# A one-tile lag behind the norm's mean, a low half moved behind four sums, and the last stores on two queues

## The chip, the cores and the metric

The kernel runs on one core of one Trainium2 chip. The metric is device time in microseconds (us) of one execution. A profile is one execution taken by the hardware profiler; it has times of its own. Engines: PE is TensorE (matmuls), DVE is VectorE, ACT is ScalarE, POOL is GpSimd, SP is SyncE. A name with a q (SPq, ACTq) is the engine's queue of transfers that it issues.

## The reference, cut to what matters

The model is one layer of a bidirectional encoder block, 1024 tokens by 1024 features, float32. Its first part (gated linear attention, a pooling branch and the gates that merge them) stands ahead of the change. The change lies in the rest:

```python
merged = jax.nn.sigmoid(g_a) * y_a + jax.nn.sigmoid(g_b) * y_b
x = x + merged @ w_out[l]                       # output projection
h2 = rmsnorm(x, norm_ffn[l])
gate, up = jnp.split(h2 @ w_ffn_in[l], 2, axis=-1)
x = x + (jax.nn.silu(gate) * up) @ w_ffn_out[l]  # gated sums
return rmsnorm(x, norm_final)
```

`rmsnorm` divides each token's row by the root of its mean square (plus 1e-6) and multiplies by a gain per feature.

## The kernel before, in words

**Products.** Every large product is split two ways. Each float32 operand is a high part, which ACT casts, and a low part, the difference, which DVE or POOL subtracts (`split_to`, L197 to 199). One step is then three matmuls of 128x128 by 128x512: high with high, high with low, low with high (`products`, L291). Above that, each product of 2 by 2 blocks is done in seven block products instead of eight (Strassen's scheme in Winograd's form); they are numbered 1 to 7 and their sums are collected block by block.

**Order.** The program is one list of instructions per engine, written out by hand; each engine works through its own in order. Small work is woven between the matmuls by `pump`, which counts matmul time and runs side generators and steps put off by `soon`.

**Output projection** (`project`, with `collect_out`, L1569). The block products run in the order 1, 4, 6, 7, 5, 2, 3. Each has two pieces c = 0, 1 of the contraction, and in each piece four groups of 128 tokens, m = 0 to 3, each with a PSUM bank of its own. Products 5, 2 and 3 start new sums (the argument `first`); three of their four banks are the same three buffers, so the first matmul of group m in one product waits until DVE has collected group m of the product before. After the last piece of group m, `collect_out` adds the bank to the residual row tile x2[t] (DVE, L1572). Rows 0 to 3 are finished in product 5, rows 4 to 7 in product 3. For a finished row tile ACT takes two sums of squares (`squares`, L1548), the tile joins the list `unnormed`, and `normed(1)` (L1562) is called, which handles all but the newest. For each tile it handles, it issues the mean's sum on DVE (L1554), the power of -0.5 on POOL (L1555), the scaling of the row tile by it on DVE (`scale_by`, L327), then the store of the tile before on SP's queue (`flush`, L500), and it lists the tile itself for the next store (`later`). Ahead of product 2 and at the end, `normed()` empties the list.

**Features.** `features(0)` starts in product 2 and `features(1)` after product 3: PE transposes the scaled tiles xn (L1503), four to a bank, ACT evicts them (L1506), ACT casts and POOL or DVE subtracts their low parts (L1484, L1488). The first of these transposes in a half reads all four tiles of that half.

**Gated sums.** The second FFN product also has seven block products in the order 1, 2, 6, 5, 3, 7, 4, each of six pieces along the contraction (`pieces`, 42 in all; the sixth is half as long). `load_piece` issues two loads, a weight w and the gated values g. `split_piece` (L1710) makes both parts of both, ACT casting, DVE taking the low part of w and POOL that of g. Splits run three pieces ahead: within each piece one is issued after the group m = 1, and two further ones behind m = 3 close to the end. Products 1, 6, 7 and 4 share the same four banks. With the last piece of product 7 (n = 35) `collect` adds each group to x2 (DVE, L1816), ACT squares that half, POOL multiplies it by the final gain (`second_half`, L1794). Product 4 closes: its first three pieces in the usual order, then for each m the last three, the sum, and `first_half` (L1801): squares, mean, power, the left half scaled on DVE (L1805), the right half on ACT (L1808), and two stores on SP's queue (L1810).

Of the kernel before, what the change touches and what calls it, by code (L numbers as in the profile page):

```python
# [17 lines left out]
P = 128  # L18
# [34 lines left out]
def kernel(  # L53
# [20 lines left out]
    nc = tc.nc  # L74
    x, out = x[0], out[0]
# [20 lines left out]
    def slot(dtype=F32, shape=(2, HALF), s="slot"):  # L96
        return slots.tile([P, *shape], dtype, tag="slot", name=name(s))
# [7 lines left out]
    def vec(width, s="v"):  # L105
        return small.tile([P, width], F32, tag="vec", name=name(s), bufs=12)

    def bank(pool, s="ps"):
        return pool.tile([P, HALF], F32, tag=pool.name, name=name(s))

    def as_f32(ap):
        return ap.bitcast(F32)
# [8 lines left out]
        out=keepf[:, :P], in_=keepf[:, :P], compare_op=ALU.is_ge, fill=0.0,  # L121
        base=0, pattern=[[1, P]], channel_multiplier=-1,
    )
    keep = const.tile([P, 4, P], U8, tag="keep", name="keep")
# [30 lines left out]
    def settle():  # L155
        while put_off:
            put_off.pop(0)[1]()
# [39 lines left out]
    def split_to(hi, lo, src, eng=nc.vector):  # L197
        nc.scalar.copy(hi, src)  # L198
        eng.tensor_tensor(lo, src, as_f32(hi), op=ALU.subtract)  # L199
# [93 lines left out]
    def mm3(ps, a, b, first, last, onto=False):  # L293
        products(ps, a, b, first, last, onto)
        pump(ps.shape[-1] / HALF)
# [30 lines left out]
    def scale_by(dst, src, rs):  # L326
        nc.vector.tensor_scalar(dst[:, :], src, rs[:, :], None, op0=ALU.mult)  # L327
# [35 lines left out]
    xn = [slot(shape=(D,), s="xn") for _ in range(4)]  # L363
# [131 lines left out]
    def later(dst, src):  # L495
        deferred.append((dst, src))

    def flush(eng=nc.sync):
        while deferred:
            eng.dma_start(*deferred.pop(0))  # L500
# [13 lines left out]
    sub = partial(nc.vector.tensor_tensor, op=ALU.subtract)  # L514
# [917 lines left out]
    x2 = [None] * NT  # L1432
# [12 lines left out]
    xn = [None] * NT  # L1445
# [99 lines left out]
    COLS = slice(0, HALF), slice(HALF, D)  # L1545

    def squares(t, ms, res, j):
        nc.scalar.activation(  # L1548
            res[:, COLS[j]], x2[t][:, COLS[j]], AF.Square, scale=1.0 / 32.0, accum_out=ms[:, j : j + 1]
        )  # L1550

    def two_scale(ms):
        rs = vec(1, "n3rs")
        nc.vector.tensor_scalar(rs[:, :], ms[:, 0:1], ms[:, 1:2], EPS, op0=ALU.add, op1=ALU.add)  # L1554
        nc.gpsimd.tensor_tensor(rs[:, :], rs[:, :], half_neg[:, :1], op=ALU.pow)  # L1555
        return rs

    mss = {}

    unnormed = []  # L1560

    def normed(keep=0):  # L1562
        while len(unnormed) > keep:
            t = unnormed.pop(0)
            scale_by(xn[t], x2[t][:, :], two_scale(mss[t]))
            flush()
            later(x2_out[t], x2[t][:, :])

# [15 lines left out]
    def before_out(p):  # L1584
        if p == 2:
            normed()
            begin(features(0), 11.5)
        elif p == 5:
            for _ in range(2):
                units[2].load()  # L1590
        elif p == 3:
            for _ in range(2):
                units_ahead.step()
# [102 lines left out]
    def load_piece():  # L1696
        if len(loaded_pieces) == len(pieces):
            return
        p, q, c = pieces[len(loaded_pieces)]
        g, w = slot(s="gor"), slot(s="wor")  # L1700
        if p in RAW_B:
            i, j = RAW_B[p]
            src = w_ffn_out[(i * PAIRS + q) * P : (i * PAIRS + q + c) * P, j * HALF : (j + 1) * HALF]
            nc.sync.dma_start(w[:, :c, :], src.rearrange("(q p) c -> p q c", p=P))
        else:
            nc.sync.dma_start(w[:, :c, :], t_out[p][:, q : q + c, :])
        nc.sync.dma_start(g[:, :c, :], g_out[p][:, q : q + c, :])
        loaded_pieces.append((w, g))

    def split_piece():  # L1710
        n = len(ready_pieces)
        if n == len(pieces):
            return
        while len(loaded_pieces) <= n:
            load_piece()
        c = pieces[n][2]
        both = []
        for src, eng in zip(loaded_pieces[n], (nc.vector, nc.gpsimd)):
            hi, lo = slot(F32R, s="oh"), slot(F32R, s="ol")
            split_to(hi[:, :c, :], lo[:, :c, :], src[:, :c, :], eng)  # L1720
            both.append((hi, lo))
        ready_pieces.append(both)

# [6 lines left out]
    for n, run in enumerate(unit_runs, 1):  # L1730
# [7 lines left out]
        for at, (of, p) in enumerate(run):  # L1738
            while n == 1 and p > 2 and p not in split_done:
                next(side[0][0])  # L1740
            units_ahead.step()
            zs[of].run(p)
            if (of, p) in ((0, 3), (1, 3)):
                units[3].load()
            elif 2 < n < FT - 1 and at in (1, 2):
                units[n + 1].load()
            if n > 1 and 0 < at + (n == 2) < 6:
                next(summing, None)
            if n == FT - 1:
                for what in early.get(at, ""):  # L1750
                    (load_piece if what == "l" else split_piece)()
            if n > 1:
                if at == 5 and n % 2 == 1 and n < FT - 3:
                    out_sums.append(OutSums((n - 1) // 2))
                if at == 5 and n == FT - 3 or at == 6 and n == FT - 2:
                    out_sums.append(OutSums(PAIRS - 2 + (n == FT - 2)))
            if p == 4:
                done[of] = zs.pop(of).g
                if of % 2:
                    put_out(of // 2, done.pop(of - 1), done.pop(of))  # L1760

    x2 = []
    gain_final = slot(shape=(D,), s="gfin")

    def load_x2():
        t = len(x2)
        if t == NT:
            nc.sync.dma_start(gain_final[:, :], norm_final[None, :].broadcast_to([P, D]))
            return
        x2.append(slot(shape=(D,), s="x2"))  # L1770
        nc.sync.dma_start(x2[t][:, :], x2_out[t])
# [29 lines left out]
    def first_half(t):  # L1801
        ms, res = scales[t]
        squares(t, ms, res, 0)
        rs = two_scale(ms)
        nc.vector.scalar_tensor_tensor(  # L1805
            res[:, COLS[0]], x2[t][:, COLS[0]], rs[:, :], gain_final[:, COLS[0]], op0=ALU.mult, op1=ALU.mult
        )
        nc.scalar.activation(res[:, COLS[1]], x2[t][:, COLS[1]], AF.Copy, scale=rs[:, :])  # L1808
        for j in range(2):
            nc.sync.dma_start(out[t * P : (t + 1) * P, COLS[j]], res[:, COLS[j]])  # L1810

    def collect(p, m, ps):

        half, j = {1: (0, 0), 2: (0, 0), 6: (0, 1), 5: (1, 1), 7: (1, 1), 3: (0, 1), 4: (1, 0)}[p]
        xs = x2[4 * half + m][:, COLS[j]]
        add(xs, ps, xs)  # L1816
        if p == 3:
            whole(m)
        elif p == 7:
            second_half(4 + m)  # L1820
        elif p == 4:
            first_half(4 + m)

    def piece_product(ps, n, m, first, last, onto):
        w, g = ready_pieces[n]
        c = pieces[n][2]
        for q in range(c):
            mm3(
                ps[:, :], tuple(t[:, q, m * P : (m + 1) * P] for t in g), tuple(t[:, q, :] for t in w),
                first and q == 0, last and q == c - 1, onto,  # L1830
            )

    n_of = len(PIECES)
# [3 lines left out]
    for at, p in enumerate(OUT_ORDER):  # L1837
        closing = at == len(OUT_ORDER) - 1
        if p in FIRST:
            banks[p in UP] = [bank(pool) for pool in (U_BANKS if p == 1 else X_BANKS)]  # L1840
        sums = banks[p in UP]
        for i in range(CLOSE if closing else n_of):
            n = at * n_of + i
            while len(ready_pieces) <= n:
                split_piece()
            load_piece()
            if n < NT + 1:
                load_x2()
            for m in range(4):
                piece_product(sums[m], n, m, i == 0 and p in FIRST, i == n_of - 1, p not in FIRST)  # L1850
                if i == n_of - 1:
                    collect(p, m, sums[m][:, :])
                if m == 1:
                    split_piece()

                if m == 3 and len(pieces) - n_of + CLOSE > n + 1 >= len(pieces) - 2 * CLOSE:
                    load_piece()
                    split_piece()
        if closing:
            settle()  # L1860
            for m in range(4):
                for i in range(CLOSE, n_of):
                    piece_product(sums[m], at * n_of + i, m, False, i == n_of - 1, p not in FIRST)
                collect(p, m, sums[m][:, :])
# [29 lines left out]
```

## Time and profile before

| what | value |
|---|---|
| median of 3 runs | 1388.93 us (1388.54 to 1389.89) |
| profiled execution, its own time | 1389.96 us |
| profiled execution, first to last instruction (span) | 1388.2 us |
| granted TensorE clock, mean | 0.999 |
| DVE, ACT, POOL busy in the span | 849.1, 624.7, 754.4 us |

In the answers on the order of time each row has a start, a length, the engine, the line, the operation, out<-in and a count of merged instructions. A bracket holds the idle time of that engine ahead of the row and the operation that ended it. A row of waits has the total of a kind of wait, the number of times and the longest.

### The profile page before, as it was taken

Reading aid. Unit: us, or ns where it says so; the run is one execution under the profiler, and the core shown is the slowest. Engines: PE = TensorE matmul, PEld = TensorE weight load, DVE = VectorE, ACT = ScalarE, POOL = GpSimd, SP = SyncE. Lnnn points to the kernel's source line nnn. Section 1 sums busy time; section 2 is a strip of 40 time slices with the busy share of each in tenths; the row PEclk is TensorE's granted clock in tenths of the full one; section 3 lists DMA queues with packets and bytes.
Section 4 is the critical chain, followed back from the end, with each engine's and each line's share of the span. In section 5 each row is a group of like instructions: output and inputs, shape, how many; then the busy total and the mean of one; then the engine's idle time right before and its main releaser. Section 6 shows DMA issues by size and latency. Waiting matters only on the chain. (4 is left out here: it accounts for less than half of the span.)

```text
span 1388.2 us, 18504 instructions
## 1 busy us (share of the span) xinstructions
PE 1363.7 (98%) x6654; PEld 1152.1 (83%) x6654; DVE 849.1 (61%) x1073; ACT 624.7 (45%) x1125; POOL 754.4 (54%) x565
## 2 busy tenths in 40 slices
PE   7999999999999999999999999999999999999997
PEld 7889899988888887888887788888888888888876
DVE  6276767767645885588784856555656556343363
ACT  6365655554334444554346533333333334453253
POOL 3260716312397546578654276666666666464364
PEclk9999999999999999999999999999999999999999
DMA  6221422321487669997416355555444447975461
GB/s 193 76 86 43 115 80 89 122 78 45 137 271 238 208 205 316 332 401 244 137 60 234 123 174 175 174 174 174 161 144 135 152 138 267 383 261 202 167 243 61
DMA packets 167452, 243.56 MB, mean 175 GB/s; under 512 B 10904, under 2 KB 97856, under 8 KB 167360
## 3 DMA queue, kind: packets, MB, share of 16 engines
q1 hardware_dynamic: 154944, 216.16, 46.8%
q10 hardware_dynamic: 12416, 26.22, 5.0%
q8 instruction: 52, 0.85, 0.3%
q14 instruction: 40, 0.33, 0.1%
HBM read 164.48 MB, written 77.86 MB: 175 GB/s over the span
## 5 line engine op out<-in xcount | busy, mean ns | idle before, releaser
L199 POOL TENSOR_TENSOR wl<-fs,wh 128x512 fp32r<-128x512 f32 x120 | 166.1, 1389 | 164.2 <-ACT wh L198 140.6
L291 PE MATMUL ps<-gl,wh 128*128 128x512 f32 x616 | 239.8, 389 | 0.8 <-DVE gl L1488 0.8
L291 PE MATMUL ps<-gh,wh 128*128 128x512 f32 x616 | 240.4, 390 | 0.0
L291 PE MATMUL ps<-gh,wl 128*128 128x512 f32 x616 | 239.7, 389 | 0.0
L199 POOL TENSOR_TENSOR wl<-fraw,wh 128x512 fp32r<-128x512 f32 x90 | 129.7, 1441 | 63.0 <-ACT wh L198 58.9
L199 POOL TENSOR_TENSOR ol<-gor,oh 128x1024 fp32r<-128x1024 f32 (+1 forms) x42 | 101.7, 2427 | 92.5 <-ACT oh L198 71.6
L199 POOL TENSOR_TENSOR wl<-raw,wh 128x512 fp32r<-128x512 f32 x44 | 64.0, 1469 | 158.8 <-ACT wh L198 158.7
L291 PE MATMUL ps<-hh,wh 128*128 128x512 f32 x376 | 149.8, 398 | 0.0
L291 PE MATMUL ps<-hh,wl 128*128 128x512 f32 x376 | 146.6, 390 | 0.0
L291 PE MATMUL ps<-hl,wh 128*128 128x512 f32 x376 | 146.5, 390 | 0.0
L291 PEld LDWEIGHTS ps<-gl,wh 128*128 128x128 f32 x616 | 115.6, 188 | 25.1 <-DVE gl L1488 1.3
L291 PEld LDWEIGHTS ps<-gh,wl 128*128 128x128 f32 x616 | 115.6, 188 | 24.0
L291 PEld LDWEIGHTS ps<-gh,wh 128*128 128x128 f32 x616 | 115.6, 188 | 23.6
L291 PE MATMUL ps<-oh,oh 128*128 128x512 f32 x308 | 119.9, 389 | 1.4 <-DVE x L1816 1.4
L291 PE MATMUL ps<-ol,oh 128*128 128x512 f32 x308 | 119.9, 389 | 0.2 <-DVE ol L199 0.2
L291 PE MATMUL ps<-oh,ol 128*128 128x512 f32 x308 | 119.8, 389 | 0.0
L199 POOL TENSOR_TENSOR wl<-wraw,wh 128x512 fp32r<-128x512 f32 x56 | 90.7, 1648 | 46.7 <-ACT wh L198 46.7
L199 DVE TENSOR_TENSOR ol<-wor,oh 128x1024 fp32r<-128x1024 f32 (+1 forms) x42 | 63.8, 1539 | 53.7 <-ACT oh L198 46.4
L198 ACT CAST wh<-fs 128x512 fp32r<-128x512 f32 x120 | 73.8, 615 | 31.4 <-DVE fs L918 25.9
L291 PEld LDWEIGHTS ps<-hh,wl 128*128 128x128 f32 x376 | 70.6, 188 | 15.0
L291 PEld LDWEIGHTS ps<-hh,wh 128*128 128x128 f32 x376 | 70.7, 188 | 13.2
L291 PEld LDWEIGHTS ps<-hl,wh 128*128 128x128 f32 x376 | 70.7, 188 | 13.2
(260 smaller groups left out, 3174.9 us busy)
## 6 DMA issues: line engine op xcount, KB each, us to landing
fraw<-in_w_ffn_in_dram SPq DMA_DIRECT2D x44, 512.0 KB, 6.4
gor<-g_out SPq DMA_DIRECT2D x35, 512.0 KB, 8.0
raw<-in_w_in_dram SPq DMA_DIRECT2D x48, 256.0 KB, 3.7
g_out<-s SPq DMA_DIRECT2D x44, 256.0 KB, 2.4
fraw<-in_w_in_dram SPq DMA_DIRECT2D x20, 512.0 KB, 4.6
wor<-t_out SPq DMA_DIRECT2D x20, 512.0 KB, 7.6
g_out<-g SPq DMA_DIRECT2D x33, 256.0 KB, 2.6
x<-in_x_dram SPq DMA_DIRECT2D x16, 512.0 KB, 4.8
```

What stands on the lines that cost most here:

```text
L198: nc.scalar.copy(hi, src)
L199: eng.tensor_tensor(lo, src, as_f32(hi), op=ALU.subtract)
L291: nc.tensor.matmul(ps, a[i], b[j], start=first and n == 0, stop=last and n == 2, skip_group_check=onto)
```

## The change

There are three edits.

First, `normed` splits its work over two lists. A tile taken off `unnormed` gets its mean's sum and its power issued and goes to the list `scaled`; all but `keep` of that list are then scaled and stored. With `keep=1` a tile is scaled one call later than its mean is issued, and its store is issued one call later too.

Second, in the last piece of product 7 (n = 35) `split_piece` stands ahead of the matmuls of m = 0 instead of behind those of m = 1, and the low part of w, DVE's subtraction, is kept back until behind the sum of m = 3. The casts and POOL's subtraction of g are issued at the new place.

Third, of the two last stores of each row tile the left half stays on SP's queue and the right half is issued by ACT.

```diff
     unnormed = []
 
+    scaled = []
+
     def normed(keep=0):
         while len(unnormed) > keep:
             t = unnormed.pop(0)
-            scale_by(xn[t], x2[t][:, :], two_scale(mss[t]))
+            scaled.append((t, two_scale(mss[t])))
+        while len(scaled) > keep:
+            t, rs = scaled.pop(0)
+            scale_by(xn[t], x2[t][:, :], rs)
             flush()
             later(x2_out[t], x2[t][:, :])
...
-    def split_piece():
+    def split_piece(lows=None):
...
         for src, eng in zip(loaded_pieces[n], (nc.vector, nc.gpsimd)):
             hi, lo = slot(F32R, s="oh"), slot(F32R, s="ol")
-            split_to(hi[:, :c, :], lo[:, :c, :], src[:, :c, :], eng)
+            if lows is None or eng is nc.gpsimd:
+                split_to(hi[:, :c, :], lo[:, :c, :], src[:, :c, :], eng)
+            else:
+                nc.scalar.copy(hi[:, :c, :], src[:, :c, :])
+                lows.append(partial(sub, lo[:, :c, :], src[:, :c, :], as_f32(hi[:, :c, :])))
             both.append((hi, lo))
...
-        for j in range(2):
-            nc.sync.dma_start(out[t * P : (t + 1) * P, COLS[j]], res[:, COLS[j]])
+        for j, eng in enumerate((nc.sync, nc.scalar)):
+            eng.dma_start(out[t * P : (t + 1) * P, COLS[j]], res[:, COLS[j]])
...
+            lows = []
+            early_split = p == 7 and i == n_of - 1
             for m in range(4):
+                if early_split and m == 0:
+                    split_piece(lows)
                 piece_product(sums[m], n, m, i == 0 and p in FIRST, i == n_of - 1, p not in FIRST)
                 if i == n_of - 1:
                     collect(p, m, sums[m][:, :])
-                if m == 1:
+                if m == 1 and not early_split:
                     split_piece()
+                if m == 3 and lows:
+                    lows.pop()()
```

## The prediction

> **What bounds the kernel now.** The page first: PE is busy for all but 24.5 us of the span, so only what lets PE start a matmul earlier, or shortens the tail behind its last one, can count.
>
> ```profile
> span 1388.2 us, 18504 instructions
> PE 1363.7 (98%) x6654; PEld 1152.1 (83%) x6654; DVE 849.1 (61%) x1073; ACT 624.7 (45%) x1125; POOL 754.4 (54%) x565
> ```
>
> Then the waits of PE over the whole span. Four rows lie where the change is or close behind it; the longer ones belong to the start of the kernel.
>
> ```profile
> PE tr L1503 <- DVE xn L327: 1.6, 1, 1.6
> PE ps L291 <- DVE x L1816: 1.4, 1, 1.4
> PE ps L291 <- DVE x L1572: 1.2, 1, 1.2
> PE ps L291 <- DVE gl L1488: 0.8, 1, 0.8
> ```
>
> Each is one wait, and each names DVE. Those on L1572 and L327 lie in the output projection, that on L1816 at the end of product 7. PE in order of time shows the three places, and two stretches without a wait (from 764.18 and 1351.82) to measure them by:
>
> ```profile
> 728.74 0.60 PE L1503 MATMUL tr<-ident,xn 128*128 128x128 f32 x4
> 730.56 0.47 PE L291 MATMUL ps<-wh,dh 128*128 128x512 f32 x1 [1.21 <-DVE x L1572]
> ...
> 752.05 0.49 PE L1503 MATMUL tr<-ident,xn 128*128 128x128 f32 x3
> 754.16 0.33 PE L1503 MATMUL tr<-ident,xn 128*128 128x128 f32 x1 [1.62 <-DVE xn L327]
> 754.26 0.47 PE L291 MATMUL ps<-gh,wh 128*128 128x512 f32 x1
> ...
> 764.18 0.60 PE L1503 MATMUL tr<-ident,xn 128*128 128x128 f32 x4
> 764.54 0.48 PE L291 MATMUL ps<-gh,wh 128*128 128x512 f32 x1
> ...
> 1351.82 0.39 PE L291 MATMUL ps<-ol,oh 128*128 128x512 f32 x1
> 1352.05 0.39 PE L291 MATMUL ps<-oh,ol 128*128 128x512 f32 x1
> 1353.85 0.50 PE L291 MATMUL ps<-oh,oh 128*128 128x512 f32 x1 [1.41 <-DVE x L1816]
> ```
>
> Matmuls overlap, so the bracket understates the loss; I go by starts. Undisturbed, the matmul behind four transposes starts 0.36 us after them (764.18 to 764.54), and one matmul follows another by 0.23. The stalls then cost 730.56 - 728.74 - 0.36 = 1.46, 754.26 - 752.05 - 0.36 = 1.85 and 1353.85 - 1352.05 - 0.23 = 1.57 us.
>
> **Edit 1, first half (product 5 into 2).** DVE in order of time:
>
> ```profile
> 721.89 0.75 DVE L327 TENSOR_SCALAR xn<-x,n3rs 128x1024 f32<-128x1024 f32 x1 [0.66 <-POOL n3rs L1555]
> 722.56 0.21 DVE L1554 TENSOR_SCALAR n3rs<-n2ms 128x1 f32<-128x1 f32 x1
> 723.43 1.81 DVE L327 TENSOR_SCALAR xn<-x,n3rs 128x1024 f32<-128x1024 f32 x1 [0.66 <-POOL n3rs L1555]
> 725.16 2.31 DVE L1202 TENSOR_TENSOR mg<-mg,mg 128x1024 f32<-128x1024 f32 x1
> 727.39 2.42 DVE L163 TENSOR_TENSOR dl<-mg,dh 128x1024 fp32r<-128x1024 f32 x2
> 729.73 2.48 DVE L1572 TENSOR_TENSOR x<-ps,x 128x512 f32<-128x512 f32 x4
> ```
>
> PE waits at 730.56 for the first of the four sums from 729.73. These follow one another without idle time although PE had long finished the first bank; they are late because DVE was busy or idling before. Ahead of each scaling DVE idles 0.66 while POOL takes the power. The row of all eight such waits:
>
> ```profile
> DVE xn L327 <- POOL n3rs L1555: 7.8, 8, 3.2
> ```
>
> One of the eight is 3.2; the other seven share 4.6, which is 0.66 each. Four stand here: 2.6 us of DVE idle time. With the lag another operation stands behind each mean: the two sums of the next group (0.6 each, by the row of four at 729.73), or the scaling of the tile before (721.89 to the next start, 0.67). Either covers 0.66. Ahead of product 2 the emptied list gives mean 3, scale 2, scale 3: covered too. No operation is added; four scalings stay four. So the four sums come 2.6 us earlier, where 1.46 is needed. Bounds: if just the last two idles go (1.3) about 0.15 us of stall is left; with all four none. The subtraction at L1202 and the two at L163 still stand ahead of the sums, and a cast of ACT between them moves up with the first. I take **1.46 us**.
>
> **Edit 1, second half (product 3 into the features).** POOL's, DVE's and ACT's order of time:
>
> ```profile
> 745.93 0.58 POOL L1555 TENSOR_TENSOR n3rs<-n3rs,half_neg 128x1 f32<-128x1 f32 x1
> ```
> ```profile
> 746.55 0.75 DVE L327 TENSOR_SCALAR xn<-x,n3rs 128x1024 f32<-128x1024 f32 x1 [3.19 <-POOL n3rs L1555]
> 747.22 0.68 DVE L1572 TENSOR_TENSOR x<-ps,x 128x512 f32<-128x512 f32 x1
> 749.35 0.68 DVE L1572 TENSOR_TENSOR x<-ps,x 128x512 f32<-128x512 f32 x1
> 752.36 1.75 DVE L327 TENSOR_SCALAR xn<-x,n3rs 128x1024 f32<-128x1024 f32 x1 [0.66 <-POOL n3rs L1555]
> ```
> ```profile
> 750.07 0.63 ACT L1548 ACTIVATE xn<-x 128x512 f32<-128x512 f32 x1 [1.41 <-DVE x L1572]
> ```
>
> Here the scaling of tile 4 waits 3.2 us, because POOL is at features' low parts until 745.93; in DVE's order the sum of group 2 (747.22) and all of tiles 5 to 7 are queued behind it. With the lag the sum of group 2 stands ahead of that scaling and is off the chain. Even if POOL comes no earlier, from tile 4's scaling at 746.55: sum of group 3 at 747.2 (0.68), ACT's squares of tile 7 from 747.95 (0.63 and about 0.2 for its read), under which tile 5 is scaled; mean 7 at 748.8, tile 6 scaled from 749.0 (0.67, covering the power), tile 7 from 749.7. That lasts 0.75 (the row of 746.55) or 1.75 (that of 752.36): it ends between 750.4 and 751.4, instead of 754.1. PE, 1.46 us ahead by the first half, wants tile 7 at 752.36 - 1.46 = 750.9. So 0 to 0.5 us of this stall stays if POOL's work does not move. It does: its low parts are made from transposes that are evicted by ACT in order behind the squares of those late sums, so it moves up by about the same 1.46 and tile 7 ends by 749.9, 1.0 ahead of PE: the stall goes. I take **1.85 us**, lower end 1.3.
>
> The stores go one call later on SP's queue. Each waits only for its tile's last sum; the last of them, behind which SP has the loads of FFN weights, waits for the sum of group 3, now about 747.9 instead of 750.0. So those loads are not pushed back. The remaining stall of the four, on L1488 (0.8), hangs on a chain of transposes, ACT and DVE that starts from PE; I let it move along unchanged.
>
> **Edit 2.**
>
> ```profile
> 1347.72 1.37 DVE L1816 TENSOR_TENSOR x<-ps,x 128x512 f32<-128x512 f32 x2 [0.39 <-PE ps L291]
> 1350.87 2.32 DVE L199 TENSOR_TENSOR ol<-wor,oh 128x1024 fp32r<-128x1024 f32 x1 [1.78 <-POOL x L1798]
> 1353.12 1.28 DVE L1816 TENSOR_TENSOR x<-ps,x 128x512 f32<-128x512 f32 x2
> ```
> ```profile
> 1344.04 1.05 ACT L198 CAST oh<-wor 128x1024 fp32r<-128x1024 f32 x1 [0.28 <-DMA wor<-t_out]
> 1345.31 1.05 ACT L198 CAST oh<-gor 128x1024 fp32r<-128x1024 f32 x1 [0.22 <-DMA gor<-g_out]
> 1349.75 1.03 ACT L198 CAST oh<-wor 128x1024 fp32r<-128x1024 f32 x1
> ```
> ```profile
> 1358.90 7.43 POOL L199 TENSOR_TENSOR ol<-gor,oh 128x1024 fp32r<-128x1024 f32 x3
> ```
>
> After two sums DVE idles 1.78 us, for the cast from 1349.75 in truth (POOL's row had ended), then takes the low part for 2.32, and only then the sums that PE stalls on. A last piece has three matmuls a group, 0.68 us, so with nothing between them the sums of groups 2 and 3 run from about 1349.1 and 1349.8 and end by 1350.5; PE wants group 2 at 1352.28. The stall of **1.57 us** goes, with 2 us to spare.
>
> What is put ahead: two casts (1.05 each) wait for transfers, which land 1.27 us apart (1344.04 to 1345.31), so w at about 1346.6 and g at 1347.9. ACT is free for the first square at 1348.9 instead of 1348.4: queued behind are squares that nobody needs before the closing. A full piece is 24 matmuls, 5.5 us, and product 4 starts two groups before the stall, at 1352.28 - 12 x 0.23 = 1349.5. DVE's low part runs from 1350.5 for up to 2.32; PE needs that piece third, at 1360.5. POOL swaps one subtraction with two multiplications, the same work, and still ends its last three subtractions at 1358.90 + 7.43 = 1366.3; PE needs the first of those at 1366.1, when only the last is not made, and the last 12 matmuls later, at 1368.8. Cost nil; the cover on POOL is 2.5 us.
>
> **Edit 3.**
>
> ```profile
> 1384.52 0.81 SPq L1810 DMA_DIRECT2D out_dram<-res  x2
> ```
> ```profile
> GB/s 0 0 0 0 0 0 0 0 0 0 0 0 133 362 438 343 381 381 419 381 343 381 438 362 381 134 0 0 0 0 0 0 0 0 0 0 0 0 0 0
> ```
>
> The first row is SP's issue of the last two stores, the second what the DMA engines moved from 1384.0 to 1388.3 in 40 slices of 0.1075 us. The two issues follow each other, 0.4 us apiece, so the second could start 0.4 earlier on ACT. But the data of both run without a gap at about 380 GB/s for 1.4 us: the second transfer already waits behind the first. Both starting together end when the two end now. Bounds -0.2 (two queues sharing less evenly) to +0.4; I take **0.1**, nearest to the data row. ACT's issues for m = 0 to 2 fall in its idle time between groups.
>
> The Trainium skill (DMA: Bandwidth & Descriptors, Issuing engines are not separate DMA queues) says that transfers issued by different engines share the same 16 DMA engines and that two issuers save only the time of issuing. By it alone the edit would bring the whole 0.4, and the sum below would be 0.3 larger.
>
> **Sum.** 1.46 + 1.85 + 1.57 + 0.1 = 4.98 us. Against the profiled execution (span 1388.2, its own time 1389.96) the span becomes 1383.2. The median shown, 1388.93, is 1.0 below that execution's time; taken from the median, **1384.0 us**. What this measurement can tell from no change is about 0.2%, 2.8 us.
>
> **Rivals.**
>
> *One of the three stalls stays* (its sum or scaling is late for another reason than the one removed). For it: DVE's operations stretch, the scaling from 0.75 to 1.8. Against: the margins worked out above, 1.1, 1.0 and 2 us. Time: 1388.93 - 3.1 to 3.5, so 1385.4 to 1385.8; 14%.
>
> *Given back at the next wait.* The stall on L1488 grows by what edit 1 wins, since its chain ends in DVE and ACT work that PE now meets 3.3 us sooner. For it: it is the next wait in time. Against: the chain begins with PE's transposes. Then only edits 2 and 3 are left: 1387.3; 7%.
>
> *Slower: POOL in front of the powers.* The power of tile 4 stands behind POOL's subtractions, and now one more sum (group 3) stands behind its scaling. If those subtractions run at the slow end of this row
>
> ```profile
> L199 POOL TENSOR_TENSOR ol<-gor,oh x42: 1287/2405/3383, 1161.4 to 1365.0; 128x1024 fp32r<-128x1024 f32 x35, 128x512 fp32r<-128x512 f32 x7
> ```
> ```profile
> 726.00:740.00 14.00, 12.79 (x70) 10.47 (x69) 6.67 (x8) 11.55 (x21) 8.21 (x6) 1.00 0.32 103
> ```
>
> (shortest, median and longest in ns; in the second row POOL's busy time is the fifth with a count), they become 3.38 / 2.41 = 1.4 times as long: 8.2 us of work from 726 to 740 and at most 5.9 more up to 745.93, so 5.6 us later. Tile 7 then ends at 751.4 + 5.6 = 757.0, a stall of 6.1 + 0.2 where 1.85 was; with the 3.1 won elsewhere the time is 1390.3. It turns the sign from 4.2 us of delay on. Against: DVE's work, which it would collide with, is no more than before. 4%, with any other loss.
>
> The Trainium skill (GPSIMD Engine Reference, 8. Key points) says that GpSimd shares its SBUF interfaces with VectorE, with contention from two-input operations there. That would fit the scalings of 1.81 us at 723.43 and of 0.75 at 721.89; no row here isolates it.
>
> *No effect:* the stalls were put down to the wrong operation: 1388.9; 3%.
>
> **How the numbers follow.** The forecast has 72%, with a range of its own from 1383.2 to 1385.0 (bounds of edit 1's second half and edit 3). Down to one stall left adds 14%, up to 1386.0 with the spread of the runs shown. The range is 1382.9 to 1386.4 and leaves out most of the other 14%. Faster by over 0.2% means below 1386.15: the first two cases less a little for one stall left and a weak tail, 83%; same 13%; slower 4%.
>
> **What would show it.** Right: no row of PE waiting on L327 at a transpose, on L1572 or on L1816; DVE's waits for POOL's power at L327 down from 7.8 us to POOL's own delay at tile 4; POOL's subtraction of piece 38 ahead of four multiplications; the data of the last stores ending as long after the last scaling as now. Wrong: any of these three rows still there, PE's wait on L1488 near 4 us, or a wait on POOL's `ol` in the closing.

## The result

The changed kernel takes 1384.54 us (median of 6 runs, 1383.96 to 1385.57); the kernel before took 1389.41 in the runs beside it (1388.39 to 1392.43). The ratio is 0.9963, 95% interval 0.9951 to 0.9975: 4.9 us less, and clear of no change. The forecast was 1384.0, or 4.93 less than the median shown then.

The profiled execution took 1385.57 us, its span is 1383.8. The page, as before with engine, busy time and instructions:

```profile
span 1383.8 us, 18503 instructions
PE 1362.2 (98%) x6654; PEld 1150.9 (83%) x6654; DVE 848.3 (61%) x1073; ACT 625.1 (45%) x1125; POOL 757.6 (55%) x565
```

Of the four waits of PE that the prediction began with, the waits of the changed kernel have one left:

```profile
PE ps L291 <- DVE gl L1488: 0.9, 1, 0.9
```

PE in order of time at the places of the first two stalls (four transposes, then the first matmul behind them):

```profile
729.00 0.60 PE L1503 MATMUL tr<-ident,xn 128*128 128x128 f32 x4
729.52 0.47 PE L291 MATMUL ps<-wh,dh 128*128 128x512 f32 x1
...
751.00 0.60 PE L1503 MATMUL tr<-ident,xn 128*128 128x128 f32 x4
751.35 0.48 PE L291 MATMUL ps<-gh,wh 128*128 128x512 f32 x1
```

The second step is 0.35 us, undisturbed. The first is 0.52, where 0.36 is undisturbed: 0.16 us of that stall is left, too little for a row of waits. DVE in order of time shows what is late, in the first half and then the second (line 1577 is line 1572 of before):

```profile
720.50 1.58 DVE L327 TENSOR_SCALAR xn<-x,n3rs 128x1024 f32<-128x1024 f32 x2 [0.22 <-POOL n3rs L1555]
721.99 2.32 DVE L1202 TENSOR_TENSOR mg<-mg,mg 128x1024 f32<-128x1024 f32 x1
724.23 4.54 DVE L163 TENSOR_TENSOR dl<-mg,dh 128x1024 fp32r<-128x1024 f32 x2
728.69 2.47 DVE L1577 TENSOR_TENSOR x<-ps,x 128x512 f32<-128x512 f32 x4
...
745.50 0.75 DVE L327 TENSOR_SCALAR xn<-x,n3rs 128x1024 f32<-128x1024 f32 x1 [2.46 <-POOL n3rs L1555]
746.17 0.68 DVE L1577 TENSOR_TENSOR x<-ps,x 128x512 f32<-128x512 f32 x1
748.08 2.46 DVE L327 TENSOR_SCALAR xn<-x,n3rs 128x1024 f32<-128x1024 f32 x2 [0.22 <-POOL n3rs L1555]
```

The waits for POOL's power are gone but for 0.22 at each end and POOL's own delay at tile 4; DVE's waits group them (7.8 in eight before):

```profile
DVE xn L327 <- POOL n3rs L1555: 2.9, 3, 2.5
```

But the pair at L163 takes 4.54 us where it took 2.42. The two scalings ahead of it take 1.58 together, where the last one alone took 1.81. Tile 7 is scaled by 748.08 + 2.46 = 750.54, ahead of PE's transposes at 751.00.

The end of product 7, DVE, POOL and ACT in order of time (line 1825 is line 1816 of before, line 1869 the low part kept back, line 1728 the cast put ahead):

```profile
1344.80 2.73 DVE L1825 TENSOR_TENSOR x<-ps,x 128x512 f32<-128x512 f32 x4
1347.45 3.00 DVE L1869 TENSOR_TENSOR ol<-wor,oh 128x1024 fp32r<-128x1024 f32 x1
```
```profile
1343.83 5.54 POOL L199 TENSOR_TENSOR ol<-gor,oh 128x1024 fp32r<-128x1024 f32 x2 [0.20 <-ACT oh L198]
1349.32 8.45 POOL L1807 TENSOR_TENSOR x<-x,gfin 128x512 f32<-128x512 f32 x4
1357.73 5.99 POOL L199 TENSOR_TENSOR ol<-gor,oh 128x1024 fp32r<-128x1024 f32 x3
```
```profile
1343.99 1.06 ACT L1728 CAST oh<-wor 128x1024 fp32r<-128x1024 f32 x1 [0.24 <-DMA wor<-t_out]
1345.22 1.06 ACT L198 CAST oh<-gor 128x1024 fp32r<-128x1024 f32 x1 [0.18 <-DMA gor<-g_out]
```

The four sums run in one go at PE's pace, the casts wait 0.2 us each for transfers, and POOL's subtraction stands ahead of its four multiplications. And the tail: the last scalings, the two issues on two queues, and what the DMA engines moved from 1379.6 to 1383.9 in 40 slices of 0.1075 us.

```profile
1379.12 0.75 DVE L1814 SCALAR_TENSOR_TENSOR res<-x,n3rs,gfin 128x512 f32<-128x512 f32 x1 [0.66 <-POOL n3rs L1555]
1379.87 0.37 ACTq L1819 DMA_DIRECT2D out_dram<-res  x1
1379.89 0.33 SPq L1819 DMA_DIRECT2D out_dram<-res  x1
```
```profile
GB/s 0 0 0 0 0 0 0 0 0 0 152 362 438 362 381 381 419 362 381 400 419 343 362 115 0 0 0 0 0 0 0 0 0 0 0 0 0 0 0 0
```

Both issues are over at 1380.2, and the data still take 1.4 us at about 380 GB/s. They end at 1382.2; the span ends 1.6 us later, where it was 1.4 before.

**One ruler for all runs.** PE runs the same 6654 matmuls in the same order in every kernel here. So the start of one matmul in a run, less the start of the same matmul in the profiled run of before, is that run's shift at that place, and a change of the shift across a stall is what the stall gained or lost. The table has these changes in us; minus is time won. The tail is given whole: from the end of DVE's drain, the instruction behind its last scaling, to the end of the span. The drain ends 0.05 us behind the scaling; from the scaling itself the two values are 3.75 and 3.95. The third column of stalls takes in 0.11 us in which PE restarts more slowly behind a stall.

| run | first stall (730.56) | second (754.26) | L1488 (768.37) | third (1353.85) | tail |
|---|---|---|---|---|---|
| before | 0 | 0 | 0 | 0 | 3.69 |
| changed | -1.29 | -1.86 | 0.00 | -1.69 | 3.90 |
| lag_only | -1.29 | -1.86 | 0.00 | -0.21 | 3.69 |
| split_only | -0.01 | -0.01 | 0.00 | -1.69 | 3.69 |
| stores_only | 0.00 | -0.02 | 0.01 | -1.08 | 3.90 |
| no_stores | -1.28 | -1.86 | 0.00 | -1.70 | 3.69 |
| lag_rows0 | -1.29 | -0.01 | 0.00 | -0.02 | 3.69 |
| lag_rows4 | 0.00 | -1.86 | -0.01 | -0.53 | 3.69 |
| low_back | 0.00 | -0.01 | 0.00 | -1.70 | 3.69 |
| split_early | 0.00 | -0.01 | 0.00 | +2.44 | 3.69 |
| pool_held | -1.45 | -1.86 | 0.01 | -1.70 | 3.69 |
| low5_early | -1.29 | -1.86 | -1.00 | -1.69 | 3.70 |
| both | -1.45 | -1.86 | -1.00 | -1.70 | 3.69 |
| last_on_sp | -1.28 | -1.86 | -0.01 | -1.70 | 3.69 |

For the changed kernel the row sums to -1.29 - 1.86 - 1.69 + 0.21 = -4.63. Edit 1 wins another 0.07 us at the transposes at 725.02, where no wait was listed; with it and smaller steps the sum from 716 us to the end is -4.73. The stages ahead of 717 us, which the change does not touch, shift by -1.3 to +2.4 us from one profiled run to another (+0.3 in the changed kernel's), so single times of whole runs cannot carry what this table can.

### The profile page after: what moved, and what is told of

Its sections match the earlier page's. It is cut to its first block, busy times and chain, and to the rows that moved or that the text cites. A ratio compares the mean times of both kernels' runs of the same rounds, so it can differ in the third digit from the quotient of the medians.

```text
span 1383.8 us, 18503 instructions
## 1 busy us (share of the span) xinstructions
PE 1362.2 (98%) x6654; PEld 1150.9 (83%) x6654; DVE 848.3 (61%) x1073; ACT 625.1 (45%) x1125; POOL 757.6 (55%) x565
## 4 chain that ended last, share of the span: by engine, by line
PE 81%; POOL 5%; issue 4%; DVE 4%; ACT 3%; DMA 2%; ACTq 0%; POOLq 0%; SPq 0%; DVEq 0%
PE ps L291 75%; POOL wl L199 2%; PE op L849 2%; DMA u_out<-uph 1%; PE kv L291 1%; PE sc L777 1%; PE op L291 1%; POOL qe L733 1%; DVE res L1796 1%; POOL wsum L637 1%; PE yb L291 1%; PE tp L1008 1%; DMA u_out<-upl 0%; DMA raw<-in_w_in_dram 0%; DVE ws L1068 0%
```

## The experiments

**The three edits apart.** Each was put alone on the kernel before, and the third was taken out of the changed kernel.

lag_only is edit 1 alone:

```diff
-            scale_by(xn[t], x2[t][:, :], two_scale(mss[t]))
+            scaled.append((t, two_scale(mss[t])))
+        while len(scaled) > keep:
+            t, rs = scaled.pop(0)
+            scale_by(xn[t], x2[t][:, :], rs)
```

> Edit 1 alone on the kernel before. Theory (each stall was DVE's order, and the edits don't touch each other): the stalls at L1572 and L327 go, that at L1816 stays at 1.4 idle; 1.3 + 1.85 = 3.15 us less, 1386.2, ratio about 0.9977. Rival (stalls are passed on, a later wait takes what an earlier one gives): less than 2 us, and the wait on L1488 or that on L1816 grows beyond 1.4.

Measured: 1386.08 us, ratio 0.9981 (0.9968 to 0.9994). The first two stalls won 1.29 + 1.86 = 3.15 us, as expected. The wait on L1488 did not grow, so nothing was passed on there.

split_only is edit 2 alone:

```diff
+                if early_split and m == 0:
+                    split_piece(lows)
...
-                if m == 1:
+                if m == 1 and not early_split:
                     split_piece()
+                if m == 3 and lows:
+                    lows.pop()()
```

> Edit 2 alone on the kernel before. Theory: only the stall at L1816 goes, 1.6 us less, 1387.8, ratio about 0.9988; the two stalls of the output projection stay. Rival (passed on): PE waits for an `ol` in the closing, and less than 0.8 us is won.

Measured: 1387.62 us, ratio 0.9988 (0.9978 to 0.9998). The third stall won 1.69 us, and the row of PE's waits on `ol` is 0.2 us, one wait, as before: nothing was passed on.

stores_only is edit 3 alone:

```diff
-        for j in range(2):
-            nc.sync.dma_start(out[t * P : (t + 1) * P, COLS[j]], res[:, COLS[j]])
+        for j, eng in enumerate((nc.sync, nc.scalar)):
+            eng.dma_start(out[t * P : (t + 1) * P, COLS[j]], res[:, COLS[j]])
```

> Edit 3 alone on the kernel before. Theory (the data bound it, and the end waits a little longer with two queues): from the end of the last DVE scaling to the end of the span 3.95 us, as in the changed kernel, against 3.75 before; the data end within 0.1 us of where they did; time the same or 0.2 us more. Rival (the second issue was on the path): 3.35 us, 0.4 us less.

Measured: 1389.71 us, ratio 1.0004 (0.9994 to 1.0015), no difference that the times can tell; by the tail 0.21 us more, the same as in the changed kernel. The issue was not on the path.

Its profile also holds a surprise: the third stall, which no edit touched, was 1.08 us shorter than in the profiled run of before. There DVE's low part had taken 2.32 us ahead of the sums. DVE and POOL of stores_only at that place:

```profile
1350.20 1.23 DVE L199 TENSOR_TENSOR ol<-wor,oh 128x1024 fp32r<-128x1024 f32 x1 [1.79 <-ACT oh L198]
```
```profile
1349.00 3.57 POOL L1798 TENSOR_TENSOR x<-x,gfin 128x512 f32<-128x512 f32 x2
1352.52 2.40 POOL L199 TENSOR_TENSOR ol<-gor,oh 128x1024 fp32r<-128x1024 f32 x1
```

Here DVE kept its pace and POOL's two multiplications took 3.57. In the kernel before they took 2.55 and DVE was slow:

```profile
1349.55 2.55 POOL L1798 TENSOR_TENSOR x<-x,gfin 128x512 f32<-128x512 f32 x2
```

The one that starts second is slowed. POOL's second multiplication, from before and then from stores_only:

```profile
1350.82 1.28 POOL L1798 TENSOR_TENSOR x<-x,gfin 128x512 f32<-128x512 f32 x1
```
```profile
1350.24 2.32 POOL L1798 TENSOR_TENSOR x<-x,gfin 128x512 f32<-128x512 f32 x1
```

Before, it starts 0.05 us ahead of DVE's low part (1350.87) and takes 1.28; in stores_only it starts 0.04 behind it (1350.20) and takes 2.32. So the third stall of a kernel without edit 2 differs from run to run: 1.57, 1.36 (lag_only), 1.04 (lag_rows4) or 0.49.

no_stores is the changed kernel without edit 3 (the diff above, reversed).

> The changed kernel without edit 3. Theory: the tail from the last DVE scaling to the end is 3.75 us again, all else as in the changed kernel: 0.2 us less than that. Rival (second issue on the path): 0.4 us more than the changed kernel.

Measured: 1384.30 us, ratio 0.9962 (0.9947 to 0.9976); the tail is 3.69 again. The medians differ by 0.24, within their scatter; the tails by 0.21, which repeats.

last_on_sp sends both stores of the very last tile through SP:

```diff
-        for j, eng in enumerate((nc.sync, nc.scalar)):
+        for j, eng in enumerate((nc.sync, nc.scalar if t < NT - 1 else nc.sync)):
```

> The changed kernel, but with both stores of the very last row tile on SP's queue; tiles 4 to 6 keep theirs on two. Theory A (the end is later because the two last transfers finish together, so that the wait for both ends later): from the end of the last DVE scaling to the end of the span 3.69 us, as with all stores on SP. Theory B (the end is later because ACT's queue was used at all in this stage): 3.90 us as in the changed kernel. PE's starts as in the changed kernel in both.

Measured in one execution: tail 3.69, so theory A. It is the last pair that counts, not that ACT's queue was in use. In the trace SP's waits for the two transfers end 2.03 and 2.68 us behind DVE's drain with one queue, and with two queues not before 2.83. With two queues both transfers run side by side and finish together and later; why their ends are reported 0.14 us later, while the data end at the same distance, stays open. The rest of the 0.21 is one more wait of 0.06 behind it.

**Edit 1 by halves.** lag_rows0 lags in product 5 alone, lag_rows4 in product 3 alone:

```diff
+    def normed(keep=0, lag=0):
...
+        while len(scaled) > lag:
...
-                normed(1)
+                normed(1, int(p == 5))    # lag_rows4: int(p == 3)
```

> On the kernel before, the lag in product 5 alone (tiles 0 to 3). Theory: PE's starts win 1.3 us at the first matmul of product 3; at the features' transposes the stall stays 1.85, since POOL, DVE and PE there all move together. Rival (one lag serves both, because the first half brings POOL's powers forward): the second stall shrinks below 1.

> On the kernel before, the lag in product 3 alone (tiles 4 to 7). Theory: the first stall stays 1.46, the second goes entirely (1.85), because tile 7 is scaled 2 us or more ahead of PE even if POOL comes no earlier. Rival (the second half needs the first): 0.5 us or more of the second stall stays.

Measured in one execution each: -1.29 and 0 in one, 0 and -1.86 in the other. The waits of PE of lag_rows0 still hold the second and third stall:

```profile
PE tr L1503 <- DVE xn L327: 1.6, 1, 1.6
PE ps L291 <- DVE x L1821: 1.4, 1, 1.4
```

The theory held in both: each half has its own stall, and the second goes without the first. The margin was smaller than expected: in lag_rows4 tile 7 is scaled by 751.85 and the transposes start at 752.36, 0.5 us and not 2. The times of whole executions cannot show these effects: 1389.22 and 1387.90 for the two, 1390.64 and 1392.22 for the next two (low_back, split_early), 1386.83 for the kernel before beside them, which alone ran from 1386.97 to 1393.66 in 26 other executions.

**Edit 2 by halves.** low_back leaves the split behind group 1 and keeps back the low part alone; split_early moves the split and keeps nothing back:

```diff
                 if m == 1:
-                    split_piece()
+                    split_piece(lows if early_split else None)   # low_back
```
```diff
+                if early_split and m == 0:
+                    split_piece()                                # split_early, no lows
```

> On the kernel before, the piece is split in its old place, behind group 1, with DVE's low part alone kept back behind the sum of group 3. Theory (the stall is DVE's place in its own order): the stall on L1816 goes as with the whole edit, 1.5 to 1.7 us of PE's starts. Rival (the cast, which came late, was the cause): 0.5 us or more of it stays.

> On the kernel before, the split stands ahead of group 0, with DVE's low part at once behind its cast. Theory: the low part then stands in front of all four sums and runs, beside POOL, until about 1350 in the time of the kernel before; the sum of group 0 ends at 1350.6 where PE wants it at 1349.5: a stall of about 1.1 us, moved to group 0. Rival (the cast's place was the cause): no stall.

Measured: low_back wins the same 1.70 as the whole edit. DVE there:

```profile
1350.69 2.47 DVE L1820 TENSOR_TENSOR x<-ps,x 128x512 f32<-128x512 f32 x4
1353.71 1.66 DVE L1862 TENSOR_TENSOR ol<-wor,oh 128x1024 fp32r<-128x1024 f32 x1 [0.55 <-ACT oh L1723]
```

The sums do not wait for the cast, which comes late; they waited only because DVE's low part stood in front of them. The earlier split is worth nothing to PE here.

split_early loses 2.44 us more than the kernel before, although the stall of 1.57 that was there is gone: some 4 us in all. DVE, PE and then the stretches (length; PE, PE's loads, DVE, ACT and POOL busy; PEclk, the granted clock, is the third figure from the end):

```profile
1348.28 2.99 DVE L199 TENSOR_TENSOR ol<-wor,oh 128x1024 fp32r<-128x1024 f32 x1 [0.34 <-ACT oh L198]
1351.20 2.47 DVE L1820 TENSOR_TENSOR x<-ps,x 128x512 f32<-128x512 f32 x4
```
```profile
1352.02 0.77 PE L291 MATMUL ps<-oh,oh 128*128 128x512 f32 x1 [2.48 <-DVE x L1820]
1352.58 0.63 PE L291 MATMUL ps<-ol,oh 128*128 128x512 f32 x1
1353.01 0.63 PE L291 MATMUL ps<-oh,ol 128*128 128x512 f32 x1
```
```profile
1350.00:1352.00 2.00, 0.00 (x0) 0.01 (x1) 2.00 (x3) 0.03 (x1) 2.00 (x2) 0.89 1.01 408
1352.00:1354.00 2.00, 1.98 (x5) 1.63 (x6) 1.67 (x3) 2.00 (x7) 2.00 (x2) 0.50 0.81 306
1354.00:1356.00 2.00, 2.00 (x8) 1.60 (x7) 0.45 (x1) 2.00 (x4) 2.00 (x3) 0.76 0.02 7
```

As expected the low part stands in front of all four sums and the stall moves to group 0, but it is 2.5 us and not 1.1: the low part ran beside POOL for 2.99 us and began later than I had put it. In that stall the granted clock fell to half, and the next six matmuls start 0.43 apart instead of 0.23, another 1.4 us.

low_back has the same far from any edit: a stall of 2.98 us in an early stage, and PE's first row behind it and the stretch show the clock at half. This is why its shift ahead of 717 is 2.4 us:

```profile
555.77 0.79 PE L291 MATMUL ps<-trh,wh 128*128 128x512 f32 x1 [2.98 <-ACT ga L1281]
```
```profile
555.80:559.20 3.40, 3.40 (x8) 2.72 (x9) 3.40 (x4) 2.20 (x4) 2.88 (x2) 0.50 0.81 301
```

**Why the first stall gave 1.29 and not 1.46.** pool_held is no_stores with POOL's two low parts of one weight piece (product 3, second half) held behind the first sum of product 2, by a copy of one column that reads that sum:

```diff
+            if hold:
+                nc.scalar.copy(hi[:, :], raw[:, k, :])
+                held.append(partial(psub, lo[:, :], raw[:, k, :], as_f32(hi[:, :])))
...
+        if p == 2 and m == 0:
+            nc.gpsimd.tensor_copy(vec(1, "hold")[:, :], xs[:, :1])
+            while held:
+                held.pop(0)()
```

> The changed kernel without edit 3, and with POOL's low parts of the second weight piece of product 3 held until behind the first sum of product 2 (one added copy of one column on POOL makes them wait). Theory (the lag gave 1.29 and not 1.46 us because two of DVE's subtractions ran beside POOL's): the pair at L163 falls from 4.5 to about 3.5 us, the sums start 1 us sooner, and PE's step from the transposes to the first matmul of product 3 is 0.36 us where it was 0.52: 0.15 us less. Rival (those subtractions are slow for another reason, the stores or the loads of weights): 4.5 us as before, no change.

Measured: 1384.10 us, ratio 0.9958 (0.9946 to 0.9969), and -1.45 at the first stall. DVE, POOL and PE:

```profile
723.47 3.45 DVE L163 TENSOR_TENSOR dl<-mg,dh 128x1024 fp32r<-128x1024 f32 x2
726.85 2.47 DVE L1583 TENSOR_TENSOR x<-ps,x 128x512 f32<-128x512 f32 x4
```
```profile
720.81 3.89 POOL L199 TENSOR_TENSOR wl<-wraw,wh 128x512 fp32r<-128x512 f32 x2 [0.28 <-ACT wh L198]
727.59 0.19 POOL L1585 COPY hold<-x 128x1 f32<-128x1 f32 x1 [2.89 <-DVE x L1583]
727.73 2.54 POOL L1587 TENSOR_TENSOR wl<-wraw,wh 128x512 fp32r<-128x512 f32 x2
```
```profile
728.23 0.60 PE L1509 MATMUL tr<-ident,xn 128*128 128x128 f32 x4
728.59 0.48 PE L291 MATMUL ps<-wh,dh 128*128 128x512 f32 x1
```

With POOL idle from 724.70 the pair falls from 4.54 to 3.45, and PE's step is 0.36, undisturbed. POOL's two held subtractions now run beside DVE's sums, which read one input from PSUM, and fall to 2.54 from 3.93 in the changed kernel:

```profile
725.99 3.93 POOL L199 TENSOR_TENSOR wl<-wraw,wh 128x512 fp32r<-128x512 f32 x2 [0.53 <-ACT wh L198]
```

So two-input subtractions on DVE and POOL hold each other up; here it is shown by holding one of them back. The Trainium skill (GPSIMD Engine Reference, 8. Key points) names contention at their shared SBUF interfaces with DVE instructions that have two SBUF inputs, and the traces agree. They show its form, too: the one that starts second waits. A low part of 128x1024 on DVE takes 1.21 to 1.23 us alone, and in all 14 traces each of the 330 that start while a two-input operation of POOL has 0.2 us or more to go ends 1.08 to 1.09 us behind it. The scalings do alike: 0.75 us alone, and in the rows of 1.81 and 1.75 the scaling starts behind a subtraction of POOL and ends 0.55 behind its end. DVE's sums from PSUM take 0.68 either way. pool_held is the best version of this study by the ruler, 0.16 + 0.21 = 0.37 us below the changed kernel; the medians, 1384.10 and 1384.54, can't tell the two apart.

**The stall that is left.** low5_early is no_stores with the second low part for FFN product 5 issued directly behind the first:

```diff
                 else:
-                    low_block(5, i, t)
+                    if i == 0:
+                        low_block(5, 0, t)
+                        hi, lo = split_b[5][1]
+                        sub(lo[:, :, :], block(0, 0, 1), as_f32(hi[:, :, :]))
+                    else:
+                        split_done.add(5)
```

> The changed kernel without edit 3, and with the second low part of the features for FFN product 5 issued directly behind the first, ahead of two other operations of DVE. Theory (the last of the four stalls is DVE's order too): the wait on L1488 (0.8) goes, PE's starts win 0.85 to 1.0 us. Rival (its chain follows PE, so the wait moves to the next low part): less than 0.3 us, and a wait on a later `gl` shows.

Measured: 1384.72 us, ratio 0.9960 (0.9947 to 0.9973). My theory fell and the rival held: at 768.37 PE won 1.00 us and gave 0.92 back at the next product, whose first low part now is the late one (DVE's row, then PE's):

```profile
768.19 3.49 DVE L1488 TENSOR_TENSOR gl<-hb,gh 128x1024 fp32r<-128x1024 f32 x3
```
```profile
769.46 0.50 PE L291 MATMUL ps<-gl,wh 128*128 128x512 f32 x1 [0.77 <-DVE gl L1488]
```

both is pool_held and low5_early together (their two diffs).

> Both of these together on the changed kernel without edit 3: 1.0 us less than it, about 1.2 less than the changed kernel; 1383.3, ratio about 0.9957. If the two were to disturb one another: not below the changed kernel without edit 3.

Measured: 1385.47 us, ratio 0.9969 (0.9957 to 0.9981): the expectation failed. Two of its parts are what the other runs showed (-1.45 at the first stall, 0.08 won at L1488 after all). The sum of 1.0 had counted on low5_early's theory, which fell. And its profile has a wait of 0.8 us on `ol` ahead of product 7's end, 0.2 to 0.3 in the others, which costs 0.52 us of PE's starts. Whether the edits have a part in that wait stays open, since nothing between them and it was changed.

## Why the prediction was right

*The three stalls are what can be won, measured by starts.* Right: 1.29, 1.86 and 1.69 against 1.46, 1.85 and 1.57. The starts were the better measure; the idle times (1.2, 1.6, 1.4) would have given 4.2.

*Edit 1, first half, 1.46.* Right in kind, 0.17 too much, and nearer to failing than it said. The step that failed: "So the four sums come 2.6 us earlier". The waits did go, all but 0.22 us of one, but the sums started at 728.69 where PE's own shift puts the old place at 729.73 + 0.25: 1.3 us earlier. The pair at L163 ran beside POOL and took 2.1 us longer, which pool_held shows by shortening it. Luck gave 1.1 back: tile 3's scaling, at 721.32, now starts ahead of POOL's subtraction (721.57) and took 0.75 instead of 1.81, which the prediction had not counted. By these figures the sums would otherwise have come some 0.2 us earlier, and most of the stall would have stayed; no run shows that case. The rival's "DVE's work, which it would collide with, is no more than before" was wrong for the same reason: no more work, but more of it at the same time as POOL's.

*Edit 1, second half, 1.85.* Right, and lag_rows4 shows it without the first half. The step "so it moves up by about the same 1.46" held in kind: POOL reached the power of tile 4 at 744.92 instead of 745.93, by about PE's own shift of 1.05 there. POOL and PE moved together, so the stall went on the margin of the lag itself. It was thinner than "1.0 ahead": tile 7 was done 0.5 us before the transposes began, about 0.8 before the fourth of them, which reads it. "2 us or more" in the later expectation was wrong.

*Edit 2, 1.57.* Right: 1.69 with the slower restart. Of its two moves the kept-back low part did it alone.

*Edit 3, +0.1.* Wrong in sign: -0.21, just past the stated bound of -0.2. The data bound it, as argued. What the sum had not in it is the end of two transfers that finish together. The prediction took 0.4 from the Trainium skill's rule (DMA: Bandwidth & Descriptors, Issuing engines are not separate DMA queues) that a second issuer saves the time of issuing. That time was saved (both issues are over 0.37 us behind the last scaling, where it was 0.83), but the rule says nothing of the end of the transfers, and nothing came of it.

*Rivals.* No stall was passed on from edit 1; POOL was not in front of the powers by more than before. The prediction left open what the scalings of 1.81 and 0.75 show, as no row isolated it; the starts beside POOL do, as above.

Sum: 4.63 by the table (4.73 with what it leaves out), 4.98 forecast, 4.9 by the medians. That the medians come nearer to the forecast is luck: their interval, 3.5 to 6.8 us, holds all of these. Part of the agreement within the table is luck too, since the first half's two errors, 2.1 too long and 1.1 too short, partly cancel.

## What to carry to other kernels

When an engine waits for a short result of another engine in the middle of its own order, put the next tile's work in between: the lag cost no operation, and 4.9 us of waits left DVE. Before counting such a gain in full, look at what the moved work will run beside, and which of the two starts first: DVE's subtraction of 1.2 us took 2.3 to 3.0 when it started behind one of POOL's. And keep a late, unneeded operation behind the sums that PE waits for; where its inputs are made matters less.

## What the runs showed of the hardware

Stalls of PE of 2.48 us (split_early) and 2.98 us (low_back) brought the granted clock to 0.50, and matmuls 0.43 us apart, for about 3.4 us. Stalls of 1.62 in the output projection, and up to 1.67 elsewhere, left it at 1.00; nothing between was seen once the clock was up. The Trainium skill (TensorE: Matmul & The Clock Gate, HAM oscillation — how this bites in real kernels) warns of gaps over about 3.4 us; these two were shorter, and the measurement decides.

Of a two-input operation on DVE and one on POOL, the one that started second ended later by about the rest of the first: 1.28 or 2.32 us for the same multiplication, by a difference of 0.1 us in the order of the starts.

Two stores of 256 KB that end the program took 0.21 us longer to be reported when issued by two engines together than by one after the other, in each of the two profiles with that pair and in none of the twelve without.
